# One of the four weight sums of each Strassen quad made by GpSimd instead of VectorE

## Chip, cores and metric

The kernel runs on one core of one Trainium2 chip. The metric is the device time of one execution in microseconds (us); the lower the better. Before the change the median of three runs is 1043.47 us (1043.3 to 1043.92).

Engines are named as the profile names them: PE is TensorE (matmuls), PEld its weight loads, DVE is VectorE, ACT is ScalarE, POOL is GpSimd, SP is SyncE, which here only starts DMAs.

## What is computed

One layer of a bidirectional encoder on 512 tokens of 1024 features, in float32:

```python
h = rmsnorm(x, g_mix); proj = h @ w_in              # 1024 x 11264
xc, gb, gc, q, k, v, g_sw, gate_a, gate_r = split(proj)
y_a = (gb * dwconv3(gc * xc)) @ w_a_out
ret = retention(rotary(q), rotary(k), v, forward) + retention(..., backward)   # 4 heads
y_r = (groupnorm(ret) * silu(g_sw)) @ w_r_out
x = x + (sigmoid(gate_a) * y_a + sigmoid(gate_r) * y_r) @ w_o
h2 = rmsnorm(x, g_ffn)
x = x + (silu(h2 @ w_ff_gate) * (h2 @ w_ff_up)) @ w_ff_down    # 2816 wide
return rmsnorm(x, g_final)
```

## The kernel before

**Split matmuls.** Every float32 operand is split into a high part (`hi`, a cast on ACT, line 171) and a remainder (`lo = src - hi`, a subtraction on DVE, line 172). A product is three matmuls, hi by hi, hi by lo and lo by hi (lines 284 to 286 plain, 325 and 369 in quads).

**Quads.** Most weight blocks are used in 2 x 2 quads by Strassen's scheme in Winograd's form: seven products in place of eight. The seven weight forms are, in this order, `b11`, `t1`, `t2`, `b21`, `t3`, `t4`, `b22` (`FORMS`). Three are loaded quarters, four are sums of quarters, and the host packs the quarters so that each sum is a plain addition of two tiles in SBUF, made in place:

- `t1`: b11 += b12; then `t2`: b11 += b22; then `t4`: b11 += b21. Each is built on the one before it, and may only be made when the form before it has been split.
- `t3`: b12 += b22, in the tile of b12. Nothing is built on it. It needs that `t1` has read b12 and that b22 has landed.

The sums are line 244, in `prefetch_form`. There are 31 sums of each kind, 124 in all: 120 on tiles of 128 x 1024 and four on 128 x 512.

**The kinds of quads.** `w` (a head's V with its swish gate, and the two branch gates; 5 quads, each form in two units), `x` (the three conv inputs; 3 quads, one unit), `a` (the conv's output product; two units), `f` (a pair of feed-forward blocks, gate and up, quads 1 to 10 with sums, one unit) and `d` (feed-forward down, after blocks 0 to 2, 3 to 6 and 7 to 10; two units). This makes 10, 3, 2, 10 and 6 sums `t3`. `prod` (line 325) makes a product of an `x` or `f` form, 24 matmuls of 256 columns; `prod_tm` (line 369) that of a `w`, `a` or `d` unit, mostly 12 matmuls of 512 columns.

**The stream of weights.** `PLAN` lists all blocks and forms in order of use. `take()` gives the next one and prepares two units further (`AHEAD = 2`), and DMAs on SP's queue run four entries further (`LEAD = 4`) into ten raw tiles. Split forms lie in `wpool`, five pairs `whi`/`wlo`. So the preparation of a form is: DMA to `raw`, sum on DVE if it is a sum, cast on ACT, subtraction on DVE, then its product on PE.

**The other work.** DVE also combines the products that are read from PSUM (lines 390, 395, 402, 1018, 1033, 1041), makes the gating (963), the forms of the activations (979 and 172 into `big`) and the transposes (185). ACT copies PSUM banks (`snap`, line 376) and applies activations. POOL makes a few tiny powers of one column (770, 891, 1099) and starts the DMAs that store intermediate results to DRAM (`store`, line 566, and the accumulating `add_y`, line 1047).

**What sets the order.** No order is written by hand. Each engine works through its queue in order, and that order is fixed when the kernel is built, by a planner that goes by dependences, by the order in the code and by its own reckoning of when things are ready. In the trace the order on DVE differs from that of the code (line 979 runs before the second line 963 of a pair, for one).

Of the kernel before, what the change touches and what calls it, by code (L numbers as in the profile page):

```python
# [15 lines left out]
ALU = mybir.AluOpType  # L16
# [126 lines left out]
def block_kernel(ctx: ExitStack, tc: tile.TileContext, xT, xtok, wpack, wquad, cols, decs, rot, g_ffn, g_final, out):  # L143
    nc = tc.nc
# [23 lines left out]
    def split(src, hi, lo, scale=None):  # L168

        if scale is None:  # L170
            nc.scalar.copy(hi, src)  # L171
            nc.vector.tensor_tensor(out=lo, in0=src, in1=hi.bitcast(F32), op=ALU.subtract)  # L172
        else:
            nc.scalar.activation(hi, src, AF.Copy, scale=scale)  # L174
            nc.vector.scalar_tensor_tensor(  # L175
                out=lo, in0=src, scalar=scale, in1=hi.bitcast(F32),
                op0=ALU.mult, op1=ALU.subtract)
# [14 lines left out]
    def unit(inbig=False):  # L192
        if inbig:
            t = bigtile(F32R)
            return t[:, 0:2, :].rearrange("p a b -> p (a b)"), t[:, 2:4, :].rearrange("p a b -> p (a b)")
        hi = wpool.tile([P, QH], F32R, tag="whi", name="whi")
        lo = wpool.tile([P, QH], F32R, tag="wlo", name="wlo")
        return hi, lo
# [22 lines left out]
    raws = {}  # L221
# [14 lines left out]
    def prefetch_form(quad, f, u, nk):  # L236


        n = nk * WIDTH[quad[0]]
        here = {"t1": "b11", "t2": "b11", "t4": "b11", "t3": "b12"}.get(f, f)  # L240
        more = {"t1": "b12", "t2": "b22", "t4": "b21", "t3": "b22"}.get(f)
        t = raws[quad, here, u][:, 0:n]
        if more:
            nc.vector.tensor_tensor(out=t, in0=t, in1=raws[quad, more, u][:, 0:n], op=ALU.add)  # L244
        hi, lo = unit()
        split(t, hi[:, 0:n], lo[:, 0:n])
        return [(hi, lo)]

    def prefetch(pieces=1, loads=None, splits=None):
        i = pos[0]  # L250
        if i >= len(PLAN):
            return False
        pos[0] += 1
        x = PLAN[i]
        load_raws(i + LEAD)
        if x[0] == "c":
            units = prefetch_block(pieces, loads, splits, x[1] == "w_o" and x[2] == 512 and x[4] == 512)
        else:
            units = prefetch_form(*x[1:])
        ready.append((x, units))  # L260
        return True
# [555 lines left out]
    for h in range(HEADS):  # L817
# [5 lines left out]
        t = sg  # L823
# [393 lines left out]
```

## Time and profile before

| | |
|---|---|
| median of three runs | 1043.47 us |
| the profiled execution | 1043.97 us |
| its span, first to last instruction | 1042.2 us |
| PE busy | 1028.3 us, 99% |
| PEld busy | 897.0 us, 86% |
| DVE busy | 875.5 us, 84% |
| ACT busy | 523.4 us, 50% |
| POOL busy | 107.7 us, 10% |
| sums of line 244, all on DVE | 148.5 us, 124 instructions |
| granted TensorE clock | 0.998 |

The profiled execution's time is its span and 1.8 us that lie around it. Busy time is the union of an engine's instructions; two DVE instructions in a row overlap by about 0.09 us, so a 1.22 us instruction moves the next one by 1.13 us. Waits are put down to whoever ended them. The table by stretches gives for each stretch its length, and then busy time and number of instructions of PE, PEld, DVE, ACT and POOL, the granted clock, the DMA share and GB/s.

### The profile page before, as it was taken

The numbers are of one execution on the slowest core, as the hardware profiler recorded it, in microseconds if no ns is written. First come the engines' busy times: TensorE is split into PE (matmuls) and PEld (weight loads), VectorE is DVE, ScalarE is ACT, GpSimd is POOL, SyncE is SP. The second block draws the span as 40 slices with busy tenths as digits, with TensorE's granted clock in tenths as the row PEclk, the third lists the DMA queues.
The fourth block names the chain that finished last, engine by engine and source line by source line (L and its number), as shares of the span: only waits on it lengthen the run. The fifth ranks groups of instructions, "written<-read, shape, count | busy, mean of one in ns | idle before, by whom it ended". The sixth has DMA issues, their size and how long they took to land.

```text
span 1042.2 us, 14832 instructions
## 1 busy us (share of the span) xinstructions
PE 1028.3 (99%) x5664; PEld 897.0 (86%) x5664; DVE 875.5 (84%) x1127; ACT 523.4 (50%) x698; POOL 107.7 (10%) x180
## 2 busy tenths in 40 slices
PE   8999999999999999999999999999999999999996
PEld 7788888888888998888888888889998999899985
DVE  6999786858787888697989998669998899889995
ACT  6546745452656545243443234355555565556553
POOL 0121111111111004202011000000002000110011
PEclk9999999999999999999999999999999999999999
DMA  9635638173645576919176535630319322663322
GB/s 325 223 117 201 236 123 281 71 254 119 199 141 182 169 284 233 341 42 358 42 283 247 205 111 173 236 113 28 92 45 275 117 85 78 193 152 102 122 35 87
DMA packets 49688, 175.07 MB, mean 168 GB/s; under 512 B 6480, under 2 KB 6480, under 8 KB 46288
## 3 DMA queue, kind: packets, MB, share of 16 engines
q1 hardware_dynamic: 36592, 131.12, 36.9%
q0 software_dynamic: 13024, 43.00, 12.9%
q8 instruction: 44, 0.72, 0.3%
q14 instruction: 28, 0.23, 0.1%
HBM read 135.56 MB, written 38.54 MB: 167 GB/s over the span
## 4 chain that ended last, share of the span: by engine, by line
PE 77%; issue 9%; DVE 7%; DMA 3%; POOL 2%; ACT 1%; SPq 0%; POOLq 0%; DVEq 0%; ACTq 0%
PE bank L369 29%; PE bank L325 27%; PE bank L285 7%; PE bank L284 7%; PE bank L286 7%; DVE wlo L172 1%; POOL z L566 1%; DVE big L185 1%; DMA big<-ql 1%; DMA big<-xT 1%; DMA z<-t 1%; DMA tab<-tab 0%; DVE big L172 0%; DVE t L464 0%; DVE big L175 0%
## 5 line engine op out<-in xcount | busy, mean ns | idle before, releaser
L171 ACT CAST whi<-raw 128x1024 fp32r<-128x1024 f32 (+1 forms) x281 | 288.6, 1032 | 302.7 <-PE bank L369 66.4
L172 DVE TENSOR_TENSOR wlo<-raw,whi 128x1024 fp32r<-128x1024 f32 (+1 forms) x281 | 335.8, 1202 | 108.8 <-ACT whi L171 107.8
L325 PE MATMUL bank<-xform,whi 128*128 128x256 f32 x1440 | 260.3, 283 | 0.0
L325 PEld LDWEIGHTS bank<-xform,whi 128*128 128x128 f32 x1440 | 224.8, 192 | 0.7 <-ACT t L376 0.6
L325 PE MATMUL bank<-xform,wlo 128*128 128x256 f32 x720 | 203.7, 283 | 0.0
L369 PE MATMUL bank<-whi,big 128*128 128x512 f32 x548 | 172.4, 390 | 0.0
L244 DVE TENSOR_TENSOR raw<-raw 128x1024 f32<-128x1024 f32 (+1 forms) x124 | 148.5, 1205 | 1.8 <-DMA raw<-wquad 0.4
L325 PEld LDWEIGHTS bank<-xform,wlo 128*128 128x128 f32 x720 | 138.2, 192 | 0.0
L369 PEld LDWEIGHTS bank<-whi,big 128*128 128x128 f32 x548 | 102.7, 188 | 22.4 <-DVE big L172 0.6
L369 PE MATMUL bank<-wlo,big 128*128 128x512 f32 x274 | 106.7, 389 | 0.0
L369 PE MATMUL bank<-whi,xform 128*128 128x512 f32 x320 | 101.2, 389 | 0.3 <-ACT t L376 0.3
L284 PE MATMUL bank<-whi,big 128*128 128x512 f32 x240 | 94.3, 395 | 1.8 <-ACT big L174 1.8
L285 PE MATMUL bank<-wlo,big 128*128 128x512 f32 x240 | 94.3, 393 | 0.0
L286 PE MATMUL bank<-whi,big 128*128 128x512 f32 x240 | 93.4, 392 | 0.0
L284 PE MATMUL bank<-big,whi 128*128 128x512 f32 x224 | 87.1, 389 | 0.0
L285 PE MATMUL bank<-big,whi 128*128 128x512 f32 x224 | 87.1, 389 | 0.0
L286 PE MATMUL bank<-big,wlo 128*128 128x512 f32 x224 | 87.1, 389 | 0.0
L376 ACT COPY t<-bank 128x512 f32<-128x512 f32 x96 | 55.5, 585 | 35.8 <-PE bank L369 17.2
L369 PEld LDWEIGHTS bank<-whi,xform 128*128 128x128 f32 x320 | 60.1, 188 | 13.1 <-ACT t L376 0.7
L369 PE MATMUL bank<-wlo,xform 128*128 128x512 f32 x160 | 62.2, 389 | 0.0
L369 PEld LDWEIGHTS bank<-wlo,big 128*128 128x128 f32 x274 | 51.4, 188 | 10.5
L284 PEld LDWEIGHTS bank<-whi,big 128*128 128x128 f32 x240 | 45.5, 190 | 12.5 <-ACT big L174 2.1
(173 smaller groups left out, 1398.6 us busy)
## 6 DMA issues: line engine op xcount, KB each, us to landing
raw<-wquad SPq DMA_DIRECT2D x124, 512.0 KB, 4.4
raw<-wpack SPq DMA_DIRECT2D x58, 512.0 KB, 4.9
z<-t POOLq DMA_DIRECT2D x24, 256.0 KB, 4.9
zform<-z POOLq DMA_DIRECT2D x6, 1024.0 KB, 6.2
v<-t POOLq DMA_DIRECT2D x16, 256.0 KB, 5.0
sg<-t POOLq DMA_DIRECT2D x16, 256.0 KB, 3.3
qh<-t POOLq DMA_DIRECT2D x16, 256.0 KB, 2.6
ql<-t POOLq DMA_DIRECT2D x16, 256.0 KB, 2.7
```

The source lines that it names most:

```text
L171: nc.scalar.copy(hi, src)
L172: nc.vector.tensor_tensor(out=lo, in0=src, in1=hi.bitcast(F32), op=ALU.subtract)
L185: nc.vector.transpose(o[:, :, :, b, :], i[:, :, :, q, :])
L244: nc.vector.tensor_tensor(out=t, in0=t, in1=raws[quad, more, u][:, 0:n], op=ALU.add)
L284: nc.tensor.matmul(ps, lh, rh, start=first, stop=False)
L285: nc.tensor.matmul(ps, lh, rl, start=False, stop=False)
L286: nc.tensor.matmul(ps, ll, rh, start=False, stop=last)
L325: nc.tensor.matmul(o, l[:, c], r[:, k], start=start and s == 0 and k == 0 and i == 0, stop=stop and k == 3 and i == 2, skip_group_check=True)
L369: nc.tensor.matmul(pss[tt], l, r[:, c], start=start and k == 0 and i == 0, stop=stop and k == n - 1 and i == 2, skip_group_check=True)
L376: nc.scalar.copy(t, ps)
L566: nc.gpsimd.dma_start(dst, t)
```

## The change

The sum `t3` is issued on GpSimd; the other three stay on VectorE. Operands, tiles and all other instructions are the same.

```diff
         t = raws[quad, here, u][:, 0:n]
         if more:
-            nc.vector.tensor_tensor(out=t, in0=t, in1=raws[quad, more, u][:, 0:n], op=ALU.add)
+
+            e = nc.gpsimd if f == "t3" else nc.vector
+            e.tensor_tensor(out=t, in0=t, in1=raws[quad, more, u][:, 0:n], op=ALU.add)
         hi, lo = unit()
         split(t, hi[:, 0:n], lo[:, 0:n])
```

## The prediction, made before the changed kernel was run

> **What bounds the kernel now.** I read the busy times first, then the table by stretches, then the waits of PE, then one feed-forward pair instruction by instruction.
>
> ```profile
> span 1042.2 us, 14832 instructions
> PE 1028.3 (99%) x5664; PEld 897.0 (86%) x5664; DVE 875.5 (84%) x1127; ACT 523.4 (50%) x698; POOL 107.7 (10%) x180
> ...
> 40.00:140.00 100.00, 100.00 (x443) 82.81 (x442) 90.10 (x103) 56.90 (x65) 14.11 (x25) 1.00 0.49 175
> 140.00:160.00 20.00, 19.70 (x87) 15.98 (x86) 16.91 (x19) 10.23 (x13) 2.17 (x4) 1.00 0.55 176
> 160.00:520.00 360.00, 360.00 (x1824) 307.98 (x1823) 287.23 (x364) 172.95 (x224) 51.20 (x88) 1.00 0.55 193
> 520.00:540.00 20.00, 19.57 (x87) 15.88 (x86) 15.93 (x29) 11.22 (x18) 2.16 (x4) 1.00 0.78 298
> 540.00:1020.00 480.00, 480.00 (x3025) 434.65 (x3024) 423.74 (x529) 239.07 (x324) 28.41 (x38) 1.00 0.43 134
> 1022.00:1042.20 20.20, 11.71 (x52) 9.38 (x50) 11.18 (x20) 6.67 (x18) 3.87 (x8) 0.89 0.28 105
> ```
>
> From 40 to 1020 us PE is busy in every microsecond but 0.30 (between 140 and 160) and 0.43 (between 520 and 540). The rest of its idle time is the start, before any sum is made, and the last 8.5 us. So the length is the number of matmuls at their own pace. The waits of PE in the whole run say the same:
>
> ```profile
> PE bank L284 <- ACT big L174: 1.8, 1, 1.8
> PE bank L493 <- ACT t L171: 1.7, 1, 1.7
> PE bank L415 <- DVE lw L508: 1.0, 1, 1.0
> PE bank L285 <- DMA big<-ql: 0.4, 1, 0.4
> PE bank L369 <- ACT t L376: 0.3, 1, 0.3
> ```
>
> Not one of them is for a weight form. The last row, 0.3 us for a copy on ACT, is the hole between 140 and 160; the DMA row is the other, and no sum touches it. What is made ahead of PE waits, in turn, for PE (waits of ACT: total, times, longest):
>
> ```profile
> ACT whi L171 <- PE bank L369: 66.4, 50, 1.7
> ...
> ACT whi L171 <- PE bank L325: 47.5, 43, 3.2
> ...
> ACT whi L171 <- DVE raw L244: 36.6, 19, 4.0
> ```
>
> A cast of a weight that waits for PE waits for a free buffer out of five: the stream of forms is as far ahead as its buffers let it be.
>
> **The change part by part.** What goes from DVE: 31 sums, a quarter of each group, 30 of the first and one of the second.
>
> ```profile
> L244 DVE TENSOR_TENSOR raw<-raw 128x1024 f32<-128x1024 f32 x120 | 145.8, 1223 | 1.8 <-DMA raw<-wquad 0.4
> L244 DVE TENSOR_TENSOR raw<-raw 128x512 f32<-128x512 f32 x4 | 2.8, 692 | 0.0
> ```
>
> That is 30 x 1.223 + 0.692 = 37.4 us of durations, some 35 us of DVE's time, since an instruction moves the next by about 1.13. None of it is on the path that sets the end; the most it can give back is the 0.30 us hole. I take 0.1 of that.
>
> One pair in the feed-forward part, where DVE is fullest, shows what the sum lies among (DVE, then ACT):
>
> ```profile
> 838.96:859.12 20.16, 20.16 (x170) 20.16 (x169) 19.01 (x25) 12.18 (x17) 0.00 (x0) 1.00 0.30 103
> ...
> 847.49 1.23 DVE L244 TENSOR_TENSOR raw<-raw 128x1024 f32<-128x1024 f32 x1
> 848.62 0.70 DVE L1018 TENSOR_TENSOR t<-bank,t 128x512 f32<-128x512 f32 x1
> 849.22 1.23 DVE L244 TENSOR_TENSOR raw<-raw 128x1024 f32<-128x1024 f32 x1
> 850.36 1.23 DVE L172 TENSOR_TENSOR wlo<-raw,whi 128x1024 fp32r<-128x1024 f32 x1
> ...
> 852.09 1.23 DVE L244 TENSOR_TENSOR raw<-raw 128x1024 f32<-128x1024 f32 x1
> 854.43 1.23 DVE L172 TENSOR_TENSOR wlo<-raw,whi 128x1024 fp32r<-128x1024 f32 x1 [1.11 <-ACT whi L171]
> ...
> 848.83 1.05 ACT L171 CAST whi<-raw 128x1024 fp32r<-128x1024 f32 x1 [2.45 <-DVE raw L244]
> 853.35 1.05 ACT L171 CAST whi<-raw 128x1024 fp32r<-128x1024 f32 x1 [2.03 <-DVE raw L244]
> 854.78 1.05 ACT L171 CAST whi<-raw 128x1024 fp32r<-128x1024 f32 x1
> 856.38 1.05 ACT L171 CAST whi<-raw 128x1024 fp32r<-128x1024 f32 x1 [0.54 <-PE bank L325]
> ```
>
> The casts come in the order t1, t2, b21, t3. The first waits for the sum at 847.49 (t1), the second for that at 852.09 (t2, which has to wait until t1 is split); so the sum at 849.22 is t3, and its cast runs at 856.38 and waits for PE. On POOL the sum can start when t1's is done, at 848.72: it has 7.7 us until its cast. Behind the cast stands more cover: the cast took the buffer of the product five units back that had just ended, so four products lie before its own, 4 x 2.88 = 11.5 us (a pair of seven takes 20.16), less 1.05 for the cast and 1.23 for the subtraction. A new wait, ACT's cast on POOL, therefore holds nothing up as long as the sum takes less than 7.7 us. If that cover went, the snap copies queued behind the cast on ACT would be late, and PE waits for those.
>
> What POOL pays. No large sum of two tiles is in this trace. The rows nearest to it:
>
> ```profile
> L530 POOL IOTA delta_i<- 128x896 int32 x1 | 0.9, 900 | 0.0
> masks.py:199 POOL TENSOR_SCALAR_AFFINE_SELECT ident<-ident 128x128 f32<-128x128 f32 x1 | 0.3, 283 | 0.0
> L449 POOL MEMSET mhalf<- 128x8 f32 x1 | 0.1, 104 | 0.0
> L509 POOL TENSOR_TENSOR lw<-lw 128x8 f32<-128x8 f32 x1 | 1.7, 1667 | 21.7 <-DVE lw L507 21.7
> L1099 POOL TENSOR_TENSOR fin<-fin,mhalf 128x1 f32<-128x1 f32 x4 | 2.2, 546 | 10.2 <-DVE fin L1097 10.2
> ```
>
> Lower end: one stream at the iota's pace, 900/896 = 1.0 ns an element, 1.0 us. With one input (the select, 283 ns for 128 elements, against 104 ns for the memset of 8) it is 179/120 = 1.5 ns; two inputs at twice that, 3.1 us, is my upper working end. The far end by rows is the power, the only two-input operation here: (1667 - 546)/7 = 160 ns an element, 164 us for a tile; a power is no addition, and I give that end 1 in 100 all the same. I take two streams at the iota's pace, 2.1 us, nearest to the rows that do little per element. 31 x 2.1 = 65 us on an engine that is busy for 108 of 1042. The Trainium skill, "GPSIMD Engine Reference" (3.1, Elementwise), gives 4497 ns for an addition of 2048 elements, which would make an estimate of 2.25 us here; the sum would come out the same by it.
>
> POOL's queue. The sum stands there among the DMAs that it starts. In the pairs there are none (0 instructions in 838.96 to 859.12); in the `w` quads a few short ones (four, 2.17 us in all, from 140 to 160). A sum ahead of a store delays it by 2.1 us, and what is stored there is read back much later; a sum behind a store that waits for DVE or ACT has its 7.7 us. SP's queue loses and gains nothing, and the raw tiles come free as before, with the casts. Price: nothing.
>
> What DVE pays back. The trace shows one thing that speaks against the change:
>
> ```profile
> 704.96 1.22 DVE L244 TENSOR_TENSOR raw<-raw 128x1024 f32<-128x1024 f32 x1
> ...
> 705.12 1.46 POOL L891 TENSOR_TENSOR ac<-ac,mhalf 128x1 f32<-128x1 f32 x1 [6.32 <-DVE ac L889]
> ```
>
> The same kind of power on one column takes 0.546 us in the row above; here it started under a DVE sum of two SBUF tiles and ended at 706.58, 0.4 us after that sum. So a POOL instruction with SBUF inputs waits for a DVE instruction with two of them. What a long POOL instruction does to DVE no row shows. Bounds: nothing, or DVE stands for the whole POOL sum. I take the second: 2.1 for 1.13, 1.0 us more for each t3 on DVE, not 1.13 less. In the pair above DVE then needs 19.01 - 1.13 + 2.1 = 19.98 of 20.16 us. That still fits, so PE keeps its pace, and the price is 0 to 0.3 us; I take 0.1. DVE's gaps, such as the 1.11 us before 854.43, are what is used up.
>
> **Sum.** Against the profiled execution (1042.2 span, 1043.97 in all): -0.1 for the hole, +0.1 for DVE, 0 for the rest: 1043.97. It lies 0.5 above the median of the runs, so against the median I forecast 1043.5 us.
>
> **The rivals.**
>
> Slower: POOL's sum locks DVE out, and the pairs become DVE-bound. The place is the feed-forward part, where DVE has least to spare. Point of decision: a sum of more than 20.16 - (19.01 - 1.13) = 2.28 us. At the upper working end, 3.1 us, eight pairs (3 to 10) lose 0.82 each, 6.6 us: 1050.1. For it: the row at 705.12, and 2.28 lies only 0.2 above my 2.1. Against it: over a whole part the limit is wider. From 798.66 to 917.64 DVE has 10.1 us to spare for six sums, 10.1/6 + 1.13 = 2.8 us each, and the lead of the forms would swallow another few us before PE felt it.
>
> ```profile
> 798.66:917.64 118.98, 118.98 (x843) 112.25 (x842) 108.87 (x127) 66.10 (x86) 6.99 (x8) 1.00 0.46 128
> ```
>
> This is the mechanism that the Trainium skill states as a rule, "SBUF — State Buffer" (SBUF: two separate sides): a VectorE instruction with two SBUF inputs and a GpSimd instruction that reads SBUF exclude each other for the whole instruction of the first, and "the other fully blocks". By that rule, the trace agrees for POOL waiting on DVE (1.46 us in place of 0.55); the other direction no row of before shows.
>
> Faster: 35 us come off DVE and something gets shorter. The holes of PE give 0.7 at most. What is left is the end:
>
> ```profile
> 1033.33 0.39 PE L369 MATMUL bank<-whi,big 128*128 128x512 f32 x1
> ...
> 1034.79 0.75 DVE L1111 SCALAR_TENSOR_TENSOR big<-big,fin,gf 128x512 f32<-128x512 f32 x1 [0.65 <-POOL fin L1099]
> 1035.46 0.68 DVE L1087 TENSOR_TENSOR big<-bank,big 128x512 f32<-128x512 f32 x1
> ```
>
> The last matmul ends at 1033.72, but DVE reads its bank only at 1035.46, because other work stands ahead in its queue. If the planner, with t3 gone from DVE, orders the end otherwise, up to 1.7 us could go; with the holes 2.4, 1041.1 us. Against it: the last t3 lies 30 us before, and nothing in the end depends on it.
>
> No effect because t3 is stuck on POOL's queue behind a store: it then comes late to its cast. That costs PE nothing below 7.7 us, and lies within "no change".
>
> **How the numbers follow.** 0.2% of 1043.5 is 2.1 us, about what can be told from no change here. Forecast, within that: 0.62. DVE locked out, slower: 0.31, most of it between 1046 and 1050, and 0.01 of it for the far end of 164 us. The end reordered, faster: 0.07. The likeliest case alone lies between 1042.5 and 1045. The range reaches down to 1041.5, little above the third case, and up to 1050, the second's price: about 4 in 100 below, 12 in 100 above.
>
> **What would show it.** Right: line 244 on POOL with 31 instructions of about 2.1 us, on DVE 93; PE busy still all of each stretch from 160 to 1020; no wait of PE on a weight; DVE instructions with two SBUF inputs of up to 3 us beside POOL's sums, and DVE's busy time up, not down, by some 30 us. Wrong: DVE's busy time down by 35 us with no longer instruction (then nothing is locked out, and the time is the same for another reason); PE waits on lines 325 or 369 for a snap, a `wlo` or a `big` of line 172, at the pairs or where a `d` quad begins (then the lock was underpriced); a POOL sum above 3.1 us. The whole is wrong if the forms' lead is not there after the planner's new order.

## The result: slower by 2.5%

| | before | after |
|---|---|---|
| median of four runs each, same chip | 1043.57 us | 1068.59 us |
| lowest to highest | 1043.30 to 1043.92 | 1067.34 to 1075.37 |
| the profiled execution, its span | 1043.97, 1042.2 us | 1069.66, 1067.9 us |

The ratio is 1.0252 (95% interval 1.0233 to 1.0272). The forecast was no change, 1043.5 us in a range up to 1050. It was wrong: the kernel lost 25 us. (The ratio is of means; one of the four runs took 1075.37 us, so it is a little above the ratio of the medians.) The new code is two lines longer, so line 244 is now 246, 325 is 327, 369 is 371 and 376 is 378.

The busy times and three of the costliest groups, after (busy us, mean ns of one, then the idle time before them):

```profile
span 1067.9 us, 14894 instructions
PE 1035.7 (97%) x5664; PEld 900.3 (84%) x5664; DVE 891.6 (83%) x1096; ACT 520.9 (49%) x696; POOL 195.0 (18%) x211
...
L172 DVE TENSOR_TENSOR wlo<-raw,whi 128x1024 fp32r<-128x1024 f32 (+1 forms) x281 | 362.5, 1298 | 114.8 <-ACT whi L171 114.2
...
L246 POOL TENSOR_TENSOR raw<-raw 128x1024 f32<-128x1024 f32 (+1 forms) x31 | 86.3, 2784 | 275.8 <-DVE raw L246 171.4
...
L246 DVE TENSOR_TENSOR raw<-raw 128x1024 f32<-128x1024 f32 x93 | 120.4, 1298 | 1.8
```

DVE has 31 instructions fewer and is busy 16 us longer. What is left on it has become slower. The waits of PE (total, times, longest) and two of the stretches shown before:

```profile
PE bank L371 <- ACT big L171: 6.0, 3, 2.8
PE bank L371 <- ACT t L378: 5.1, 5, 2.5
PE bank L327 <- ACT t L378: 5.0, 4, 1.3
PE bank L286 <- ACT big L174: 1.9, 1, 1.9
PE bank L912 <- DVE t L897: 1.7, 1, 1.7
```

```profile
40.00:140.00 100.00, 96.72 (x426) 79.44 (x425) 88.67 (x95) 53.07 (x62) 23.53 (x29) 1.00 0.47 165
...
540.00:1020.00 480.00, 468.24 (x2942) 423.40 (x2941) 420.49 (x493) 229.69 (x312) 78.02 (x52) 0.99 0.43 135
```

PE was busy in all of both stretches; now it has holes of 3.3 and 11.8 us there. Almost 20 us of waits stand in these five rows. The fourth was there before (line 284, 1.8 us); the others are new but for 0.3 us. None of them is for a weight form: PE waits for a snap (`t`, line 378), for a split activation (`big`, line 171) or for the gating of the conv (line 897). From the start of the first matmul to the end of the last, the same 5664 matmuls took 1058.0 us, against 1032.7 before. These 25.4 us are nearly the whole 25.7 by which the span grew.

**What happens on DVE.** Four places of the timeline (start, duration, engine, line, operation):

```profile
123.22 2.40 POOL L246 TENSOR_TENSOR raw<-raw 128x1024 f32<-128x1024 f32 x1
124.26 0.69 DVE L621 TENSOR_TENSOR t<-bank,rcs 128x512 f32<-128x512 f32 x1 [1.22 <-PE bank L288]
...
130.51 2.40 POOL L246 TENSOR_TENSOR raw<-raw 128x1024 f32<-128x1024 f32 x1 [4.89 <-DVE raw L246]
130.90 3.09 DVE L172 TENSOR_TENSOR wlo<-raw,whi 128x1024 fp32r<-128x1024 f32 x1
...
294.16 1.22 DVE L172 TENSOR_TENSOR wlo<-raw,whi 128x1024 fp32r<-128x1024 f32 x1
294.33 3.31 POOL L246 TENSOR_TENSOR raw<-raw 128x1024 f32<-128x1024 f32 x1 [0.71 <-DVE raw L246]
295.41 3.31 DVE L246 TENSOR_TENSOR raw<-raw 128x1024 f32<-128x1024 f32 x1
```

The POOL sum of two tiles takes 2.40 us when nothing is in its way. In that time a DVE instruction that reads one operand from PSUM runs as usual (0.69 us at 124.26). One that reads two tiles from SBUF stands until POOL is done: at 130.90 a subtraction that takes 1.22 us elsewhere takes 3.09, and ends 1.08 us after POOL's sum. At 294.33 both directions are seen: POOL first waits for the subtraction before it, 3.31 us in place of 2.40, and the DVE sum behind it then waits for POOL, 3.31 in place of 1.22. The longest POOL sum, at 859.30, took 7.13 us: DVE ran instructions with two SBUF operands without a gap, and by the times POOL came in only when one that reads PSUM began (line 1020, at 864.08): from there to its end are 2.35 us, a sum's own time. There are 28 held instructions on DVE, none of which reads PSUM. Against the usual duration of their kind they lose 48.7 us, and the sums taken away were worth 30 us of DVE's busy time (875.5 before, 845.2 in the kernel without them, below).

**How that reaches PE.** The first `w` quad. The first fence is the changed kernel, the second the same place of a kernel that leaves the sum out and has the same order on every engine (the first experiment below; its lines are two lower):

```profile
62.91 2.71 POOL L246 TENSOR_TENSOR raw<-raw 128x1024 f32<-128x1024 f32 x1 [4.74 <-DVE raw L246]
69.05 2.39 POOL L246 TENSOR_TENSOR raw<-raw 128x1024 f32<-128x1024 f32 x1 [3.42 <-DVE raw L246]
...
63.40 2.71 DVE L538 TENSOR_SCALAR scr<-delta,lgam 128x896 f32<-128x896 f32 x1
...
69.49 3.02 DVE L172 TENSOR_TENSOR wlo<-raw,whi 128x1024 fp32r<-128x1024 f32 x1
...
85.84 1.21 DVE L246 TENSOR_TENSOR raw<-raw 128x1024 f32<-128x1024 f32 x1
...
87.14 1.05 ACT L171 CAST whi<-raw 128x1024 fp32r<-128x1024 f32 x1 [3.46 <-DVE raw L246]
...
89.56 1.06 ACT L378 COPY t<-bank 128x512 f32<-128x512 f32 x2
...
90.18 0.50 PE L371 MATMUL bank<-whi,xform 128*128 128x512 f32 x1 [2.48 <-ACT t L378]
```

```profile
64.31 0.69 DVE L536 TENSOR_SCALAR scr<-delta,lgam 128x896 f32<-128x896 f32 x1
...
68.56 1.22 DVE L172 TENSOR_TENSOR wlo<-raw,whi 128x1024 fp32r<-128x1024 f32 x1
...
83.10 1.21 DVE L244 TENSOR_TENSOR raw<-raw 128x1024 f32<-128x1024 f32 x1
...
84.40 1.05 ACT L171 CAST whi<-raw 128x1024 fp32r<-128x1024 f32 x1 [3.46 <-DVE raw L244]
...
86.82 1.06 ACT L376 COPY t<-bank 128x512 f32<-128x512 f32 x2
```

Two DVE instructions are held, 2.71 for 0.69 and 3.02 for 1.22, together 3.8 us. Before the first of them the changed kernel is 0.92 us ahead of the other in this trace (63.40 for 64.31). DVE works almost without a gap here, so 15 us later a sum on DVE starts 2.74 us late (85.84 for 83.10): DVE has lost 3.7 us. The cast that waits for it is as late (87.14 for 84.40), the snap behind that cast in ACT's queue too (89.56 for 86.82), and PE, which needs the snap's bank, stands from 87.7 to 90.2. Nothing here waits for POOL's result.

In a feed-forward pair the same happens within 5 us. A sum runs on POOL from 837.42 to 839.95:

```profile
837.59 2.90 DVE L172 TENSOR_TENSOR big<-t,big 128x512 fp32r<-128x512 f32 x1
...
842.32 0.58 ACT L378 COPY t<-bank 128x512 f32<-128x512 f32 x1
...
842.95 0.51 PE L327 MATMUL bank<-xform,whi 128*128 128x256 f32 x2 [1.33 <-ACT t L378]
```

The split of an activation takes 2.90 us where it takes 0.68 elsewhere; the cast of the next one, the snap behind that cast and PE follow. 2.2 us on DVE became 1.5 us of PE by the spacing of its matmuls, here and twice more (at 966 and 988): the room was 0.7 us. In the `w` quad above PE lost 2.65 us of DVE's 3.7, so the room was 1.0.

At the start of a `d` quad the way is shorter:

```profile
888.71 2.83 DVE L172 TENSOR_TENSOR wlo<-raw,whi 128x1024 fp32r<-128x1024 f32 x1
...
892.94 3.26 POOL L246 TENSOR_TENSOR raw<-raw 128x1024 f32<-128x1024 f32 x1 [2.48 <-DVE raw L246]
...
893.97 3.31 DVE L246 TENSOR_TENSOR raw<-raw 128x1024 f32<-128x1024 f32 x1
...
899.88 0.68 DVE L965 TENSOR_TENSOR t<-t,t 128x512 f32<-128x512 f32 x1
...
900.59 1.29 ACT L171 CAST big<-t 128x512 fp32r<-128x512 f32 x2 [1.13 <-DVE t L965]
...
901.26 0.79 PE L371 MATMUL bank<-whi,big 128*128 128x512 f32 x1 [2.78 <-ACT big L171]
901.85 0.63 PE L371 MATMUL bank<-wlo,big 128*128 128x512 f32 x1
```

Two instructions are held, a subtraction for 1.6 us (888.71, beside a POOL sum from 887.19 to 890.46) and a sum for 2.1 (893.97), and DVE has no gap between them or behind, so all of it is 3.7 us late. Both are for weights, but behind them on DVE stands the gating (line 965) of the very activations that the quad's products multiply. PE waits 2.78 us for their cast; by the spacing of its matmuls it lost 2.94, so the room was 0.8 us. Then it runs slower: 0.63 us for a matmul that took 0.39. That is the granted clock, here in two stretches of the changed kernel; both were at 1.00 before:

```profile
700.00:720.00 20.00, 18.18 (x117) 16.63 (x116) 15.80 (x23) 11.88 (x22) 4.35 (x3) 0.92 0.22 71
900.00:920.00 20.00, 18.74 (x76) 15.16 (x77) 16.41 (x19) 11.21 (x14) 2.41 (x1) 0.91 0.35 108
```

After three of the stalls (at 715, 785 and 901 us) the clock was halved for 3.4 us, which costs 1.7 us each time: some 5 us of the 25.7 are the clock, the other 20 the stalls themselves.

### The profile page after: what moved, and what is told of

It is laid out like the page before. It is cut to its first block, busy times and chain, and to the rows that moved or that the text cites. A ratio compares the mean times of both kernels' runs of the same rounds, so it can differ in the third digit from the quotient of the medians.

```text
span 1067.9 us, 14894 instructions
## 1 busy us (share of the span) xinstructions
PE 1035.7 (97%) x5664; PEld 900.3 (84%) x5664; DVE 891.6 (83%) x1096; ACT 520.9 (49%) x696; POOL 195.0 (18%) x211
## 4 chain that ended last, share of the span: by engine, by line
PE 55%; issue 18%; DVE 17%; POOL 3%; DMA 3%; ACT 3%; SPq 0%; POOLq 0%; DVEq 0%; ACTq 0%
PE bank L371 24%; PE bank L327 16%; PE bank L286 5%; PE bank L287 5%; PE bank L288 5%; DVE wlo L172 5%; DVE raw L246 2%; DVE big L172 2%; POOL z L568 1%; ACT whi L171 1%; DVE big L185 1%; DVE t L965 1%; DMA big<-ql 1%; DVE t L981 1%; DVE t L622 1%
## 5 line engine op out<-in xcount | busy, mean ns | idle before, releaser
L172 DVE TENSOR_TENSOR wlo<-raw,whi 128x1024 fp32r<-128x1024 f32 (+1 forms) x281 | 362.5, 1298 | 114.8 <-ACT whi L171 114.2
L246 POOL TENSOR_TENSOR raw<-raw 128x1024 f32<-128x1024 f32 (+1 forms) x31 | 86.3, 2784 | 275.8 <-DVE raw L246 171.4
L371 PEld LDWEIGHTS bank<-whi,big 128*128 128x128 f32 x548 | 104.0, 190 | 31.2 <-ACT big L171 7.2
L246 DVE TENSOR_TENSOR raw<-raw 128x1024 f32<-128x1024 f32 x93 | 120.4, 1298 | 1.8
```

What stands on the lines that cost most here:

```text
L246: e.tensor_tensor(out=t, in0=t, in1=raws[quad, more, u][:, 0:n], op=ALU.add)
L371: nc.tensor.matmul(pss[tt], l, r[:, c], start=start and k == 0 and i == 0, stop=stop and k == n - 1 and i == 2, skip_group_check=True)
```

## The experiments

Three explanations stood against each other: POOL's sum keeps DVE's two-operand instructions out of SBUF (the lock, theory L); the planner's new order (122 of DVE's instructions and 61 of ACT's have moved against before) is a worse one (O); ACT's casts wait for a sum that is slow on POOL (W). In all of the experiments the times are medians, and ratios are of means, to the kernel before on the same chip.

**The new order alone.** Before, with the sum `t3` left out altogether. The order on PE, DVE and ACT is that of the changed kernel, but for one of DVE's subtractions (at 270 us).

```diff
-        if more:
+        if more and f != "t3":
```

> Leaves t3's sum out altogether (t3 is then b12 alone); the order on PE, DVE, ACT and SP is that of the changed kernel, POOL has 31 instructions fewer. Theory L (a POOL sum that reads SBUF keeps DVE's instructions with two SBUF inputs out, and they come late to the casts and snaps): 1041 to 1045 us, as before the change, with DVE's busy time 35 us below before and no DVE instruction longer than 1.25 us. Rival O (the planner's new order on DVE and ACT is worse): 1060 to 1070. Rival W (ACT's cast waits too long for the slow POOL): 1041 to 1045.

1043.74 against 1043.02 us, 1.0004 (0.9995 to 1.0013).

```profile
span 1042.5 us, 14806 instructions
PE 1029.1 (99%) x5664; PEld 897.5 (86%) x5664; DVE 845.2 (81%) x1096; ACT 521.3 (50%) x696; POOL 108.2 (10%) x180
```

The order costs nothing, so it isn't the cause. And DVE's 30 us of relief are worth nothing either: with PE busy throughout, less work on DVE shortens nothing. (For the same reason a relief can't have hidden a worse order: PE had next to no hole that it could have closed.)

**POOL as slow, but without reading.** As the change, with three `memset`s on the tile of `t3` in place of the sum, which is left out. Same order again.

```diff
+            if f == "t3":
+                for _ in range(3):
+                    nc.gpsimd.memset(t[:, 0:n * 13 // 16], 0.03)
+            else:
```

> In place of t3's sum POOL writes b12's tile three times with a constant (13/16 of it each time, about 2.4 us in all), reading nothing; ACT's cast still waits for POOL. Same order on PE, DVE, ACT and SP as the changed kernel. Theory L: no lock without reads, 1041 to 1045 us. Rival O: 1060 to 1070. Rival W: 1060 to 1070, since POOL is as late as in the changed kernel.

1045.11 us, 1.0016 (1.0007 to 1.0026).

```profile
L247 POOL MEMSET raw<- 128x832 f32 x90 | 72.0, 805 | 233.2 <-DVE raw L249 136.5 <-ACT big L171 35.4 <-issue 30.0
```

Three times 805 ns, 2.4 us, is as long as the undisturbed sum, at the same place in POOL's queue, and the casts wait for it as they would for the sum. At most 0.26% of the 2.5% can be this wait. What is missing is the reading of SBUF, and with it the held instructions: none with two SBUF operands is left.

**The lock alone.** Before, with all four sums on DVE, and once the tile of `t3` is split and dead, POOL adds it to itself. Nobody reads the result, and PE, DVE and ACT keep the order of before, but for two of DVE's subtractions. One thing does wait for POOL: a tile is free for its next load only when POOL is done with it, and 28 of SP's loads wait for line 248.

```diff
         split(t, hi[:, 0:n], lo[:, 0:n])
+        if f == "t3":
+            nc.gpsimd.tensor_tensor(out=t, in0=t, in1=t, op=ALU.add)
```

> The kernel before, t3 on DVE, with a sum on POOL besides, of t3's dead tile with itself once t3 is split; nobody reads it. Order on PE, DVE and ACT as before the change. Theory L: slower than the changed kernel, 1065 to 1095 us, since DVE now pays the 1.9 us for each sum and has no 1.13 us taken off. Rivals O and W: 1043 to 1046.

1055.83 us, 1.0125 (1.0110 to 1.0140).

```profile
PE bank L327 <- ACT t L378: 5.0, 5, 1.7
PE bank L371 <- ACT t L378: 2.9, 1, 2.9
...
L248 POOL TENSOR_TENSOR raw<-raw 128x1024 f32<-128x1024 f32 x30 | 66.3, 2211 | 312.0 <-DVE wlo L172 248.0 <-issue 35.2 <-ACT big L171 25.3
```

A sum that nobody needs costs 13 us, less than was expected, and PE's waits for a snap are back. It holds 31 instructions of DVE for 34.4 us in all (DVE's busy time is 906.9 us, up by 31.4), about 70% of the change's 48.7 us. One reason that it is less is that the sum is shorter: with the same tile as both inputs it takes 1.89 us undisturbed. The other is its place: nine of the held instructions are caught only in its last part, for less than 0.5 us each, since it runs where DVE waits for a cast.

Not all of the 13 us need be the lock. The longest stall, 2.9 us at 106 us, and the 1.7 us of half clock behind it come after two holds of 1.6 us each; but just before it DVE waits 2.0 us for a store (line 544) that SP started 2.5 us later than before, behind loads that waited for POOL.

**The same place, writing only.** As the one before, with three `memset`s for the sum. Here 26 loads wait for POOL. Twelve of DVE's instructions and six of ACT's stand elsewhere in the order than before, nearly all of them between 100 and 155 us.

```diff
+        if f == "t3":
+            for _ in range(3):
+                nc.gpsimd.memset(t[:, 0:n * 13 // 16], 0.03)
```

> As the run with the idle sum, but POOL writes the dead tile three times with a constant (about 2.4 us) and reads nothing. All theories: 1043 to 1046 us; if it is slower, it is POOL being busy that costs (its DMA starts come late), not its reading.

1043.75 us, 1.0009 (0.9999 to 1.0018): no cost that can be told from none. POOL was busy 181.7 us, longer than in the kernel with the dead sum (176.3). So it is not POOL's being busy, and not the loads that wait for it: it is POOL's reading. Only for the stall at 106 us, where the order differs, is this run no exact counterpart.

**The sum by DMA.** POOL only starts a DMA that adds the second quarter onto the first as it is loaded. The order is that of the changed kernel, but for one of DVE's subtractions.

```diff
+            if f == "t3":
+                i = next(j for j, x in enumerate(LOADS) if x[1:4] == (quad, more, u))
+                nc.gpsimd.dma_start(out=t, in_=wquad[i][:, 0:n], accum_op=ALU.add)
+            else:
```

> t3's sum made by an accumulating DMA (b22 read a second time from DRAM and added into b12's tile) that POOL only starts; same order on PE, DVE, ACT and SP as the changed kernel, 31 DMAs and some 16 MB more. Theory L: nothing on POOL reads SBUF, so no lock; DVE is relieved as in the run without the sum, which gave no gain: 1042.5 to 1046 us. If DVE's relief were worth something once the lock is gone: below 1041.

1043.02 against 1042.60 us, 1.0001 (0.9991 to 1.0010).

```profile
PE 1027.9 (99%) x5664; PEld 897.1 (86%) x5664; DVE 845.9 (81%) x1096; ACT 521.0 (50%) x696; POOL 136.0 (13%) x211
...
L247 POOL DMA_DIRECT2D raw<-wquad x31 | 27.6, 890 | 261.0 <-DVE t L984 76.6 <-DVE raw L249 74.9 <-ACT whi L171 56.2
```

This is the change's purpose without the lock: the whole `t3` off DVE, in the changed order, with the sum made elsewhere, and no instruction of DVE held. It is neither slower nor faster than before.

**The places.** The change for one kind of quad at a time: `w` (10 sums), `x` and `a` (5), `f` (10), `d` (6).

```diff
+            e = nc.gpsimd if f == "t3" and quad[0] in "w" else nc.vector
```

> Only the ten sums t3 of the w quads on POOL, the other 21 on DVE. Theory L, priced place by place from the changed kernel's trace (stalls at 87, 106, 151, 212 and 272 us, 5.9 us in all, of which some 0.5 were there before): 1047 to 1050 us. If the price goes by the number of sums (25 us over 31): 1051.

> Only the five sums t3 of the x and a quads on POOL. The same locks as in the changed kernel (DVE instructions of 1.9 to 2.7 us), but no stall of PE lay near them there. Theory L by place: 1042.5 to 1044.5 us, no change. By the number of sums: 1047.

> Only the ten sums t3 of the feed-forward pairs on POOL. Theory L by place (stalls at 713, 753, 841, 966, 988 and 1017 us in the changed kernel, 8.2 us, and some 1.7 us for a TensorE clock that falls to one half for a while behind the first): 1049 to 1054. By the number of sums: 1051.

> Only the six sums t3 of the down quads on POOL, which lie where the gating of the last pair must be ready for the next product with nothing to spare. Theory L by place (stalls at 782, 898 and 1024 us in the changed kernel, 6.5 us, and 3.4 us for two falls of the clock): 1050 to 1055. By the number of sums: 1048.

| sums on POOL | ratio (95%) | lost, us | DVE held, us |
|---|---|---|---|
| `w`, 10 | 1.0049 (1.0032 to 1.0065) | 5.1 | 13.6 |
| `x`, `a`, 5 | 1.0001 (0.9992 to 1.0011) | 0.1 | 6.2 |
| `f`, 10 | 1.0085 (1.0067 to 1.0102) | 8.9 | 20.1 |
| `d`, 6 | 1.0085 (1.0070 to 1.0100) | 8.9 | 10.2 |
| all, 31 (the change) | 1.0252 (1.0233 to 1.0272) | 26.3 | 48.7 |

(Lost: the ratio less one, times 1043.5.) The parts add up to 23 us of the change's 26, so there is no large effect of all together. But the price goes by place, not by number. Five sums in `x` and `a` quads hold DVE for 1.2 us each and cost nothing. DVE has gaps there that take it up (in the 50 us shown it is busy for 43), and PE stays full:

```profile
325.00:375.00 50.00, 50.00 (x385) 48.34 (x384) 42.98 (x41) 24.88 (x30) 9.76 (x8) 1.00 0.56 209
```

The six sums of the `d` quads hold DVE for less than those of the `w` quads and cost more, nearly as much as they hold: at the start of two of the quads two holds in a row stop PE for 2.8 and 2.9 us, each time followed by 3.4 us at half clock.

```profile
PE bank L371 <- ACT big L171: 6.7, 3, 2.8
```

**Shorter holds.** First the sum on POOL in four pieces of 256 columns, so that DVE can get in between; then half of the tile on POOL and half on DVE.

```diff
+                for c in range(0, n, 256):
+                    nc.gpsimd.tensor_tensor(out=t[:, c:c + 256], in0=t[:, c:c + 256],
+                                            in1=raws[quad, more, u][:, c:c + 256], op=ALU.add)
```

> The changed kernel with each sum on POOL in pieces of 256 columns (four, or two for the narrow tile); same order on PE, DVE, ACT and SP. If what costs is that one DVE instruction stands for a whole sum (up to 2.2 us at once), the pieces let DVE in between and the time falls to 1045 to 1055 us. If what costs is the whole time that DVE loses, and each piece locks in its turn, it stays at 1065 to 1075 or more.

```diff
+                m = n // 2
+                for e, sl in ((nc.gpsimd, slice(0, m)), (nc.vector, slice(m, n))):
+                    e.tensor_tensor(out=t[:, sl], in0=t[:, sl], in1=raws[quad, more, u][:, sl], op=ALU.add)
```

> Half of each sum t3 on POOL, the other half on DVE: locks of about 1.2 us, and half as much taken off DVE. Theory L with little room before PE waits (a few tenths to 1.2 us at the stalls of the changed kernel): the stalls of 0.8 to 1.5 us nearly vanish and those of 2 to 3 us shrink to about half and no longer bring the clock down: 1045 to 1055 us. In proportion to the lock: 1056.

The pieces: 1062.91 against 1042.60 us, 1.0191 (1.0176 to 1.0206). Halves: 1052.65, 1.0093 (1.0078 to 1.0108). The pieces lie between the two times that were expected. They mostly do let DVE in: 75 of the holds are 0.6 us or less. But two subtractions stood for three and four pieces in a row, 2.2 and 2.7 us (at 334.08 and 301.15), and 77 instructions are held in place of 28, 39.5 us in all: a piece takes 0.73 us undisturbed, four of them 2.9, longer than the sum in one. Half a sum on POOL holds DVE for 22.5 us and loses 9.7 us. It ran in an order of its own, with 85 of DVE's instructions elsewhere than in the changed kernel, so that figure isn't the size alone. In the kernels with much held time the loss is between 0.38 and 0.54 of it: 26.3 of 48.7 (the change), 19.9 of 39.5 (pieces), 13.0 of 34.4 (dead sum), 9.7 of 22.5 (halves), 8.9 of 20.1 (`f`), 5.1 of 13.6 (`w`). That is a count over these runs, no law; the `x` and `d` quads lie on either side of it.

**One input in place of two.** Before, with two additions of a constant on the dead tile by POOL.

```diff
+        if f == "t3":
+            for _ in range(2):
+                nc.gpsimd.tensor_scalar_add(t, t, 1.0)
```

> As the run with the idle sum of a dead tile, but POOL adds a constant to it, twice, with one SBUF input instead of two. Order of before. If any read of SBUF by POOL locks DVE's two-input instructions out: 1048 to 1060 us, like the idle sum (1055.8). If only POOL's two-input instructions do: 1043 to 1045.

1064.05 us, 1.0205 (1.0189 to 1.0220). It doesn't answer the question that it was made for. An addition of a constant takes 2.77 us, so a pair of them keeps POOL busy for 5.6 us, and four in a row held up more than DVE once:

```profile
91.49 13.47 POOL L249 TENSOR_SCALAR raw<-raw 128x1024 f32<-128x1024 f32 x4 [3.79 <-DVE wlo L172]
...
105.84 0.42 SPq L545 DMA_DIRECT2D tab<-tab  x1
...
113.92 0.69 DVE L541 TENSOR_SCALAR tab<-delta,lgam 128x896 f32<-128x896 f32 x1 [11.60 <-DMA tab<-tab]
...
PE bank L372 <- ACT t L379: 11.0, 1, 11.0
```

SP's loads waited up to 7.7 us here for tiles that POOL was still using. The store of line 545, behind them in SP's queue, started at 105.84, 7.7 us later than before. DVE waited 11.6 us for it, ACT for DVE, and PE from 106.3 on for a snap on ACT, 11 us, followed by a slow clock. So more than half of the 21 us has another mechanism than the lock: POOL keeps tiles from being loaded. What the run does show is that one input also holds DVE, but for less: 23.8 us in 35 instructions, beside 187 us of POOL's.

## Why the prediction was wrong

**What bounds the kernel: right.** PE was the bound, and taking work off DVE is worth nothing: leaving the sum out altogether gives 1.0004. The 0.30 us hole was never to be had.

**POOL's sum: 2.1 us forecast, 2.40 measured alone and 2.78 in the mean,** as it has to wait for DVE as well. The estimate from the Trainium skill, "GPSIMD Engine Reference" (3.1 Elementwise), 2.25 us, was the nearer one. The size of the sum did not decide: with 2.40 in the forecast's own sum for a pair, DVE's 19.01 - 1.13 + 2.40 is 20.28 against 20.16 us, a loss of 0.12 for eight pairs, 1 us. With the mean of 2.78 it would be 4 us. The `f` quads alone lost 8.9.

**The wait of ACT on POOL: right.** No wait of ACT for line 246 on POOL stands among its waits, and the `memset`s of the same length bound it at 0.26%. **POOL's queue and SP's: right,** nothing was lost there, as the writes alone show.

**What DVE pays back: the step that failed.** "I take the second: 2.1 for 1.13" had the mechanism, DVE standing for all of POOL's sum. Its price, 0.1 us, came from comparing DVE's total need with the pair's length, 19.98 of 20.16 us, and from "that still fits, so PE keeps its pace". The gaps of DVE are not a stock from which a delay can be paid. They lie where they lie, each ended by a cast on ACT or a product on PE, and until the next of them all that stands behind the held instruction is late by 0.9 to 2.2 us. Holds with no gap between them add up, to 3.7 us in the first `w` quad, where they were carried for 15 us to PE, and to 3.7 at the `d` quad shown.

The same step named the wrong cover. The lead of weight forms (7.7 us, and four products behind it) is real, and no wait of PE is for a weight. But DVE's and ACT's queues carry other work between the weights: the gating, the split of activations, the snaps. These are made just in time, with a room of 0.7 to 1.0 us at the three places shown. The prediction named this branch among its signs, PE waiting on a snap or on a `big` where a `d` quad begins: "then the lock was underpriced". That is what the rows show, but it stood as a sign and had no price.

**The rival "slower": right in mechanism and sign, wrong in size and place.** It put the loss in the pairs, as DVE-bound work, at 6.6 us with a 3.1 us sum. The sums took less than that in the mean (2.78 us), and the loss was four times as large: of the parts, 8.9 lie in the `f` quads, 8.9 in the six sums of `d` and 5.1 in `w`, where the rival had none. And no term of the forecast held the 5 us of half clock.

The Trainium skill, "SBUF — State Buffer" (SBUF: two separate sides), states the rule that the forecast took as its case. It says that a VectorE instruction with two SBUF inputs, or one in a two-port mode, and a GpSimd instruction exclude each other, the first holding the ports for its whole length, and that for two SBUF inputs this goes against a GpSimd instruction that reads SBUF. The runs agree for two inputs: 3.09 us for 1.22 beside the sum, and no instruction with two SBUF operands held beside the `memset`s. Beside an addition of a constant the hold did not last for the whole instruction; there the measurement decides (last section). The forecast went wrong in the price, not in the rule.

**The signs.** 31 sums on POOL and 93 on DVE: as said. DVE instructions of up to 3 us: 3.42 (a subtraction at 746.67). DVE's busy time up by 30 us: up by 16, because only 28 instructions were caught, each for 1.7 us in the mean. PE busy throughout: no. The faster rival, an end in another order, didn't come: from PE's last matmul to the end of the span it is 8.8 us, against 8.5.

No version is faster than before. The sum by DMA is as fast, and it frees 30 us of DVE for which nothing waits.

## What to carry to other kernels

A held instruction in an in-order queue delays everything behind it; price it by the tightest consumer behind it and by the distance to the queue's next gap, not by whether the engine's total still fits. Where PE is full, look for what is made just in time for it (here snaps and gated activations, with a room of a microsecond or less at the places shown), since lead in one stream doesn't cover another stream in the same queue. And work given to POOL beside a DVE full of two-input SBUF instructions isn't free: in this kernel a sum by DMA or a write cost nothing, a sum that reads SBUF cost 0.8 us apiece. Work on POOL also keeps its tiles from being loaded again.

## What was unexpected of the hardware

- Stalls of PE of 1.9, 2.1 and 2.9 us were each followed by 3.4 us at half the granted clock, while one of 2.65 us at 87 us was not, though one of the same length at the same place was in the kernel with only the `w` sums; and a stall of 1.9 us at 31 us in the kernel with the `memset`s on `t3` was not either, nor was the stall for the conv's gating, 1.9 us in both, in the kernel with only the `f` sums. The Trainium skill, "TensorE: Matmul & The Clock Gate" (Part 1: The HAM clock gate), speaks of idle windows of about 3.4 us that run free of the kernel. Free-running windows fit those that were spared, and 3.4 us of slow clock is what was seen, but shorter gaps than a window were enough here.
- A one-input instruction of DVE can be held as well: line 538, 2.71 us in place of 0.69, at 63.40 beside a POOL sum. The `memset`s hold such instructions too, though none with two inputs: 1.18 us in place of 0.68 (line 541, at 64.09, `memset`s on `t3`) and 1.30 (line 539, at 91.92, `memset`s on the dead tile).
- A POOL addition of a constant to 128 x 1024 takes 2.77 us, longer than the sum of two tiles (2.40), and holds DVE for a part of its time only: a DVE subtraction that started 1.27 us after it ran unhindered. No run shows why.
